# Token factors of three RMS norms taken out of the normalised rows and applied later: in gate and up of the two FFNs, and in the scale of the cross attention's exponential

## The chip, the core and the metric

The kernel runs on one core of one Trainium2 chip. The metric is device time in microseconds (us) of one execution. The core's engines work side by side and wait for one another by semaphores: TensorE (PE, matrix products into PSUM banks), VectorE (DVE), ScalarE (ACT), GpSimd (POOL), and SyncE (SP), which here issues almost all DMA transfers. Each engine runs its own instructions in the order in which they were written to its queue.

## What is computed

One layer of an encoder over 1088 tokens (1024 prompt frames and 64 frames of a running stream), 1024 features wide. Cut to what the change touches:

```python
def rmsnorm(x, g):
    xf = x.astype(F32)
    y = xf * lax.rsqrt(jnp.mean(xf * xf, axis=-1, keepdims=True) + EPS)
    return (y * g.astype(F32)).astype(x.dtype)

def swiglu(x, w_gu, w_d):
    gate, up = jnp.split(x @ w_gu, 2, axis=-1)
    return (jax.nn.silu(gate) * up) @ w_d

def ffn_half(x, g, w_gu, w_d):
    return x + 0.5 * swiglu(rmsnorm(x, g), w_gu, w_d)

def cross_attend(h, g_cross, w_cq, w_co, mk, mv):
    q = (rmsnorm(h, g_cross) @ w_cq).reshape(bsz, L, N_MEM_HEADS, MEM_HEAD_DIM)
    s = jnp.einsum('bqhd,bkhd->bhqk', q.astype(F32), mk.astype(F32)) * (MEM_HEAD_DIM ** -0.5)
    p = jax.nn.softmax(s, axis=-1)
    o = jnp.einsum('bhqk,bkhd->bqhd', p, mv.astype(F32)).reshape(bsz, L, D_MODEL)
    return o.astype(h.dtype) @ w_co

# per layer: ffn_half (FFN1), mixing (S5 group and differential attention, w_out),
# cross_attend into 256 memory tokens, ffn_half (FFN2), final rmsnorm
```

An RMS norm multiplies each token by one factor (the reciprocal root of its mean square) and each feature by one weight g. A matrix product over features is linear, so the token factor can be multiplied in before the product or after it.

## The kernel before

Activations lie with features on the 128 partitions: eight rows of 128x1088 (`row()`, one pool of 36 buffers) hold all tokens, in two column halves `TH[0]` and `TH[1]` of 544, called c = 0 and 1. Every product is made in fp32r from a high and a low part of each operand (`mm3`: high*high, high*low, low*high). A weight tile of 128x512 is cast on ACT (L154, and L155 for a rounded copy) and its low part subtracted on DVE (L156); an activation operand is cast on ACT (L343) and its low part made on DVE or POOL (L348).

**An FFN** (`ffn`) runs over 22 columns j of 128 hidden features. Per j, gate and up are made by seven products of half size in Strassen's manner, named b11, b21, t1, t2, t3, t4 and b22. Each is 24 matmuls of 272 columns, so 168 per j. b11, b21 and b22 take quarters of the input rows as they are; t1 to t4 take sums and differences of quarters, made on DVE (L338, class `Operands`). The weights of t1, t2, t3 and b22 are mixed on POOL (L605 to L608, `mixed`). `second()` adds the products into `gate` and `up` from PSUM (L580 on ACT, L585 on DVE) and on POOL (L635, L636), takes Silu of gate (L643, ACT), multiplies it into up (L644, POOL) and stores the row to `hid_d`. At an FFN's start the products b11 and b21 of the first `SKEWS` columns are made ahead of everything else, ten products where SKEWS is 5, while the operands of t1 to t4 are still being made. A side chain (`side`: in FFN1 the S5 parameters, `s5_prep`, and lambda) is advanced one step per product.

**Norm of FFN1.** Token tiles of x are loaded, squared and summed (`x_square`, L834 on ACT, L836 on DVE), and the factor is made per token (`half_rstd`, L218 to L230) and spread over all partitions by transposes of a broadcast column (L140 into L302, L303), giving the row `rb0`. Squares and factors stand ahead of all else in a hand-ordered block. Then, for each row and half, x is transposed on PE, copied to SBUF (`keep`, L863, L864) and multiplied by g and by rb0 in one DVE instruction (`x_norm`, L871).

**Norms 2 and 3** (class `Normed`: ahead of the cross attention, and ahead of FFN2). As the residual rows come out of the output projection's squares (`square`, steps n = 0 to 7), `add` squares them on ACT (L537) and sums them on POOL (L538). `finish(c)` makes sums over partitions with PE, then the factors, then the spread row. `get(k, c)` multiplies a row half by g and the spread row in place on DVE (L558): 16 for norm 2, 16 for norm 3. For norm 2, half c = 1 is normalised during `mem_proj` (the memory keys, L1658 on PE); the operands of w_cq's product follow (L425, L429, L454 on DVE). For norm 3, rows go to `Operands` of FFN2.

**Cross attention.** `c_scores` takes a maximum per token (L1753, L1754) and an exponential with the constant scale 1/16 (L1758).

Outside a few hand-ordered blocks, a tile scheduler sets each engine's order from its own timeline.

## Time and profile before

| | us |
|---|---|
| median of 3 runs | 2438.22 (2432.18 to 2440.07) |
| profiled execution | 2436.29 |
| its span, first to last instruction | 2434.5 |
| PE busy | 2272.9 (93%) |
| DVE busy | 1666.4 (68%) |
| ACT busy | 1287.2 (53%) |
| POOL busy | 1027.4 (42%) |

The mean granted TensorE clock was 0.977 of full speed. Busy shares are means over stages that differ: in the long middle of each FFN, PE is busy throughout; where a norm stands between two stages, PE stands idle in pieces. A row of the chain of waits or of a timeline that ends in square brackets gives the idle time of the engine just before that instruction and what ended it: "[8.52 <-DVE wl L156]" is 8.52 us until DVE wrote wl at line 156.

### The profile page before, as it was taken

The numbers are of one execution on the slowest core, as the hardware profiler recorded it, in microseconds if no ns is written. First come the engines' busy times: TensorE is split into PE (matmuls) and PEld (weight loads), VectorE is DVE, ScalarE is ACT, GpSimd is POOL, SyncE is SP. The second block draws the span as 40 slices with busy tenths as digits, with TensorE's granted clock in tenths as the row PEclk, the third lists the DMA queues.
The fourth block names the chain that finished last, engine by engine and source line by source line (L and its number), as shares of the span: only waits on it lengthen the run. The fifth ranks groups of instructions, "written<-read, shape, count | busy, mean of one in ns | idle before, by whom it ended". The sixth has DMA issues, their size and how long they took to land. (4 is left out here: it accounts for less than half of the span.)

```text
span 2434.5 us, 45373 instructions
## 1 busy us (share of the span) xinstructions
PE 2272.9 (93%) x16926; PEld 2207.6 (91%) x16926; DVE 1666.4 (68%) x3749; ACT 1287.2 (53%) x2511; POOL 1027.4 (42%) x801
## 2 busy tenths in 40 slices
PE   6899999999999998989989799987999999999998
PEld 6899999998999997978889799887999999998997
DVE  6557544358899696269978888789743333369897
ACT  6554444446555322267856566655554445464543
POOL 2666777754144200035335320355564445434340
PEclk9899999999999999999999999999999999999999
DMA  6232444443412425433443411133232222262312
GB/s 208 71 112 80 114 112 119 114 177 134 144 42 99 145 81 162 132 125 105 139 148 119 149 53 43 64 110 102 62 107 76 80 80 76 76 220 87 117 46 92
DMA packets 268295, 263.16 MB, mean 108 GB/s; under 512 B 36477, under 2 KB 217770, under 8 KB 268074
## 3 DMA queue, kind: packets, MB, share of 16 engines
q1 hardware_dynamic: 267984, 260.24, 33.6%
q8 instruction: 133, 2.18, 0.4%
q14 instruction: 88, 0.72, 0.1%
q10 hardware_dynamic: 90, 0.02, 0.0%
HBM read 187.03 MB, written 68.58 MB: 105 GB/s over the span
## 5 line engine op out<-in xcount | busy, mean ns | idle before, releaser
L174 PE MATMUL b<-r,wh 128*128 128x272 f32 (+4 forms) x9600 | 1690.6, 297 | 63.1 <-DVE r L709 14.5
L174 PEld LDWEIGHTS b<-r,wh 128*128 128x128 f32 x9600 | 1425.2, 192 | 79.8 <-DVE r L709 18.8
L174 PE MATMUL b<-r,wl 128*128 128x272 f32 (+4 forms) x4800 | 1055.0, 297 | 33.1 <-DVE wl L156 33.1
L174 PEld LDWEIGHTS b<-r,wl 128*128 128x128 f32 x4800 | 786.6, 191 | 37.3 <-DVE wl L156 37.0
L585 DVE TENSOR_TENSOR r<-b,r 128x272 f32<-128x272 f32 x440 | 172.2, 434 | 259.6 <-PE b L174 239.6
L156 DVE TENSOR_TENSOR wl<-wr,q 128x512 fp32r<-128x512 f32 x304 | 207.2, 682 | 192.7 <-ACT q L155 86.5
L154 ACT CAST wh<-wr 128x512 fp32r<-128x512 f32 x304 | 188.1, 622 | 248.6 <-PE b L174 224.8
L155 ACT CAST q<-wr 128x512 fp32r<-128x512 f32 x304 | 179.8, 591 | 259.7 <-DVE wl L156 257.4
L454 DVE TENSOR_TENSOR r<-r,r 128x544 fp32r<-128x544 f32 x224 | 213.2, 969 | 25.3 <-ACT r L453 24.2
L436 POOL TENSOR_TENSOR ws<-r,r 128x512 f32<-128x512 f32 x32 | 51.2, 1604 | 318.1 <-PE b L140 134.8
L154 ACT CAST wh<-ws 128x512 fp32r<-128x512 f32 x158 | 98.0, 621 | 137.6 <-PE b L174 114.6
L156 DVE TENSOR_TENSOR wl<-ws,q 128x512 fp32r<-128x512 f32 x158 | 107.5, 680 | 80.9 <-PE b L174 55.9
L155 ACT CAST q<-r 128x512 fp32r<-128x512 f32 x146 | 86.4, 592 | 124.0 <-DVE wl L156 123.7
L453 ACT CAST r<-r 128x544 fp32r<-128x544 f32 x224 | 143.8, 649 | 11.0 <-DMA r<-hid_d 6.5
L709 DVE SCALAR_TENSOR_TENSOR r<-b,r 128x272 f32<-128x272 f32 (+4 forms) x328 | 132.4, 438 | 22.2 <-PE b L174 21.2
L635 POOL TENSOR_TENSOR r<-r,r 128x544 f32<-128x544 f32 x44 | 61.4, 1395 | 195.8 <-DVE r L585 166.2
L155 ACT CAST q<-ws 128x512 fp32r<-128x512 f32 x158 | 93.8, 594 | 86.2 <-DVE wl L156 79.5
L156 DVE TENSOR_TENSOR wl<-r,q 128x512 fp32r<-128x512 f32 x146 | 99.5, 681 | 31.5 <-ACT q L155 30.2
L605 POOL TENSOR_TENSOR ws<-wr,wr 128x512 f32<-128x512 f32 x44 | 57.5, 1306 | 145.7 <-DMA wr<-w_ffn_gu 131.2
L1383 POOL CAST r<-r 64x256 fp32r<-64x256 f32 x32 | 13.6, 424 | 249.4 <-PE b L140 237.0
L644 POOL TENSOR_TENSOR r<-r,r 128x1088 f32<-128x1088 f32 x44 | 111.8, 2542 | 10.0 <-ACT r L643 10.0
L140 PE MATMUL b<-ident,r 128*128 128x128 f32 (+4 forms) x649 | 93.3, 281 | 19.8 <-DMA r<-g_subln 10.1
(323 smaller groups left out, 2942.3 us busy)
## 6 DMA issues: line engine op xcount, KB each, us to landing
wr<-w_ffn_gu SPq DMA_DIRECT2D x196, 256.0 KB, 2.9
hid_d<-r SPq DMA_DIRECT2D x44, 544.0 KB, 2.8
r<-hid_d SPq DMA_DIRECT2D x44, 544.0 KB, 6.7
h_d<-r SPq DMA_DIRECT2D x48, 272.0 KB, 2.4
r<-h_d SPq DMA_DIRECT2D x48, 272.0 KB, 2.8
r<-w_ffn_d SPq DMA_DIRECT2D x24, 512.0 KB, 7.1
wr<-w_in SPq DMA_DIRECT2D x32, 256.0 KB, 2.7
wr<-w_ffn_d SPq DMA_DIRECT2D x20, 256.0 KB, 2.8
```

The costliest lines, as they stand in the source:

```text
L140: T.transpose(out, in_, ident[:n, :n])
L154: A.copy(hi, x)
L155: A.copy(r, x)
L156: V.tensor_tensor(out=lo, in0=x, in1=r.bitcast(F32), op=ALU.subtract)
L174: T.matmul(pc[:, :c1 - c0], w, x[:, c0:c1], start=(first + i == 0 and q == 0), stop=(first + i == n - 1 and q == 2))
L453: A.copy(r[:, 0], v)
L454: V.tensor_tensor(out=r[:, 1], in0=v, in1=r[:, 0].bitcast(F32), op=ALU.subtract)
L585: V.tensor_tensor(out=oc, in0=pc, in1=tc_, op=ALU.add)
L605: G.tensor_tensor(out=s1, in0=r[2], in1=r[3], op=ALU.add)
L635: G.tensor_tensor(out=gate[:, T2], in0=gate[:, T2], in1=up[:, T2], op=ALU.add)
L644: G.tensor_tensor(out=up, in0=up, in1=gate, op=ALU.mult)
L709: V.scalar_tensor_tensor(out=hc_, in0=pc, scalar=0.5, in1=hc_, op0=ALU.mult, op1=ALU.add)
```

## The change

In FFN1, x_norm multiplies by g alone, with an instruction of one tensor operand. In norms 2 and 3, `get` multiplies by g alone, on ACT. The token factor is then applied:

- in both FFNs inside `second()`: up times the spread row `rb()` on POOL ahead of the product b22, and gate times it on DVE ahead of Silu, one instruction of 128x1088 each per j, 44 of each in all;
- in the cross attention as the scale of the exponential, per token (`by_tile` gives it as a 128x9 column set, from nine small products with ones; no spread row for norm 2).

With that, the factors are due later. FFN1's squares move out of the hand-ordered block into `x_start`, between the other steps, and the factors come after the operands of t1 and t2. Norm 2's `get` moves into steps 2, 5 and 6 of the square, the other four halves and `by_tile` into the background of mem_proj. Norm 3's rows become operands of b11 and b21 in steps 5 and 6; its factors come behind the operands of t1 and t2. SKEWS goes from 5 to 4 for both FFNs: eight products ahead instead of ten, and one gate row fewer, while the spread row is held through each FFN. The side chain of FFN1 takes lambda first.

```diff
-SKEWS = 5, 5
+SKEWS = 4, 4
...
-                V.scalar_tensor_tensor(out=x, in0=x, scalar=self.g[k], in1=self.rb[:, TH[c]], op0=ALU.mult, op1=ALU.mult)
+                A.activation(x, x, AF.Copy, scale=self.g[k])
             return self.rows[k]
 
-    def ffn(ops, w_gu, w_d, src_d, between, side=iter(()), ordered=False, on_row=None, on_chunk=None):
+        def by_tile(self):
+
+            ssq, acc = small([P, 9], "ssq"), self.acc.rearrange("p c n -> p (c n)")
+            V.memset(ssq, 1.0)
+            for t0, t1 in ((0, 4), (4, 8), (8, 9)):
+                p = bank()
+                for t in range(t0, t1):
+                    n = P if t < 8 else NS
+                    T.matmul(p[:n, (t - t0) * P:(t - t0 + 1) * P], acc[:, t * P:t * P + n], ones, start=True, stop=True)
+                n = P if t0 < 8 else NS
+                V.tensor_copy(ssq[:n, t0:t1], p.rearrange("p (t n) -> p t n", n=P)[:n, 0:t1 - t0, 0])
+            return rsqrt_mean(ssq, D, [P, 9], "rs")
+
+    def ffn(ops, w_gu, w_d, src_d, rb, between, side=iter(()), ordered=False, on_row=None, on_chunk=None):
...
             add(prod(w_split(r[3]), "t4"), up[:, T1])
+            G.tensor_tensor(out=up, in0=up, in1=rb(), op=ALU.mult)
             aside(j)
             yield
             add(prod(w_split(s[3]), "b22"), gate[:, T2])
             aside(j)
             yield
+            V.tensor_tensor(out=gate, in0=gate, in1=rb(), op=ALU.mult)
             A.activation(gate, gate, AF.Silu)
...
-        V.scalar_tensor_tensor(out=x0[k][:, TH[c]], in0=kept[k, c], scalar=g_ffn1[k], in1=rb0[:, TH[c]],
-                               op0=ALU.mult, op1=ALU.mult)
+        V.tensor_scalar(out=x0[k][:, TH[c]], in0=kept[k, c], scalar1=g_ffn1[k], scalar2=None, op0=ALU.mult)
...
-                if c == 0 and k in RS1_AT:
-                    next(rs1)
+                if c == 0 and k < 5:
+                    x_square(0, k, SQ_ACT[k])
+                elif c == 0 and k > 5:
+                    for t in ((0, 1, 2), (3, 4))[k - 6]:
+                        x_square(1, t, SQ_ACT[t])
             if c == 0:
                 yield
                 for k in range(X_AHEAD):
                     keep(k, 1)
+        for c in range(2):
+            yield from half_rstd(ssq0[c], rb0, c)
...
     def h2_norm():
         yield from steps(H2_PAUSE)
-        for _ in norm2.finish(1):
-            yield from steps(2)
-        for k in range(KT):
+        for k in range(4):
             norm2.get(k, 1)
-            if k % 2:
-                yield
+            yield
+        r = norm2.by_tile()
+        V.tensor_scalar(out=r, in0=r, scalar1=1.0 / 16, scalar2=None, op0=ALU.mult)
+        rs2.append(r)
...
-        A.activation(pe[:n], p[:n, :256], AF.Exp, bias=mx[:n], scale=1.0 / 16, accum_out=ss[:n])
+        A.activation(pe[:n], p[:n, :256], AF.Exp, bias=mx[:n], scale=rs, accum_out=ss[:n])
...
     def co_step(n, i):
-        if 4 * n + i in N0_AT:
-            next(n0, None)
-        if n == 6 and i:
-            ops3.get("b11", i - 1)
+        if n == 5:
+            ops3.get("b11", i)
+        if n == 6:
+            ops3.get("b21", i)
...
     def h_start():
-        yield from steps(H3_PAUSE)
-        yield from norm3.finish(1)
...
         ops3.low(*prev)
+        yield
+        for c in range(2):
+            yield from norm3.finish(c)
```

How the engines' own order changes, at three places. In these rows r, wh, wl, wr, ws, q and b are tiles with their numbers (r_97 is the spread row of FFN1), then the shape.

ACT at FFN1's start, before: seven squares (L834), then the first weight cast (L154) and the copies of the spread row (L302, L303).

```order
L834 ACTIVATE r_133,xq_119<-r_106 32x1024
L282 COPY gc<-b_89 128x45
L220 ACTIVATE rht_138<-rhv_135 128x5
L834 ACTIVATE r_146,xq_121<-r_108 128x1024
L834 ACTIVATE r_148,xq_121<-r_110 128x1024
L834 ACTIVATE r_150,xq_121<-r_117 32x1024
L154 CAST wh_201<-wr_199 128x512
L302 COPY r_97<-b_156 128x512
L303 COPY r_97<-b_157 128x32
```

The same engine now, around the first weight cast (L149), and some 20 instructions later:

```order
L845 ACTIVATE r_188,xq_119<-r_98 128x1024
L875 COPY r_195<-b_125 128x32
L874 COPY r_195<-b_190 128x512
L149 CAST wh_161<-wr_159 128x512
...
L338 CAST r_305<-r_303 128x544
L845 ACTIVATE r_308,xq_121<-r_108 128x1024
L845 ACTIVATE r_310,xq_121<-r_110 128x1024
L845 ACTIVATE r_312,xq_121<-r_112 128x1024
L215 ACTIVATE rht_714<-rhv_711 128x5
L150 CAST q_361<-wr_357 128x512
L338 CAST r_316<-r_314 128x544
```

Three copies of x and one operand cast now stand ahead of the first weight cast, and six squares stand behind it, among the weight casts and the operand casts of b11 and b21.

POOL in FFN1, where the columns j = 0 and 1 end their t4 and begin b22 (L348: low parts of operands, L605 to L608: weight mixes, L644: Silu's product), before:

```order
L348 TENSOR_TENSOR r_1124<-r_583,r_1124 128x544
L606 TENSOR_TENSOR ws_1084<-ws_1083,wr_1075 128x512
L607 TENSOR_TENSOR wr_1079<-wr_1075,wr_1079 128x512
L608 TENSOR_TENSOR ws_1085<-wr_1077,ws_1084 128x512
L348 TENSOR_TENSOR r_1189<-r_330,r_1189 128x544
L348 TENSOR_TENSOR r_1207<-r_349,r_1207 128x544
L605 TENSOR_TENSOR ws_1375<-wr_1371,wr_1373 128x512
```

And now (L343: low parts, L614 to L617: weight mixes, L647: the new product with the spread row):

```order
L343 TENSOR_TENSOR r_1051<-r_543,r_1051 128x544
L615 TENSOR_TENSOR ws_1011<-ws_1010,wr_1002 128x512
L616 TENSOR_TENSOR wr_1006<-wr_1002,wr_1006 128x512
L617 TENSOR_TENSOR ws_1012<-wr_1004,ws_1011 128x512
L647 TENSOR_TENSOR r_765<-r_765,r_97 128x1088
L647 TENSOR_TENSOR r_800<-r_800,r_97 128x1088
L343 TENSOR_TENSOR r_1118<-r_289,r_1118 128x544
L614 TENSOR_TENSOR ws_1306<-wr_1302,wr_1304 128x512
L615 TENSOR_TENSOR ws_1307<-ws_1306,wr_1298 128x512
L616 TENSOR_TENSOR wr_1302<-wr_1298,wr_1302 128x512
L617 TENSOR_TENSOR ws_1308<-wr_1300,ws_1307 128x512
L343 TENSOR_TENSOR r_1136<-r_314,r_1136 128x544
```

The two low parts of b22 that POOL makes stood back to back right behind the weight mixes; now two products with the spread row stand ahead of the first, and four further mixes ahead of the second.

DVE at the end of the memory keys' mem_proj (L156: low part of a weight; L425, L429: operands of w_cq), before:

```order
L156 TENSOR_TENSOR wl_16605<-wr_16602,q_16606 128x512
L558 SCALAR_TENSOR_TENSOR r_14715<-r_14715,gc,r_16052 128x544
...
L558 SCALAR_TENSOR_TENSOR r_14722<-r_14722,gc,r_16052 128x544
L156 TENSOR_TENSOR wl_16639<-wr_16636,q_16640 128x512
L425 TENSOR_TENSOR r_14715<-r_14715 128x544
```

And now (L151: low part of a weight; L449, L420, L424: operands of w_cq):

```order
L151 TENSOR_TENSOR wl_16546<-wr_16543,q_16547 128x512
L449 TENSOR_TENSOR r_16734<-r_14755,r_16734 128x544
L449 TENSOR_TENSOR r_16743<-r_14756,r_16743 128x544
L420 TENSOR_TENSOR r_14755<-r_14755 128x544
L449 TENSOR_TENSOR r_16752<-r_14757,r_16752 128x544
L420 TENSOR_TENSOR r_14756<-r_14756 128x544
L449 TENSOR_TENSOR r_16761<-r_14758,r_16761 128x544
L424 TENSOR_TENSOR r_14755<-r_14759,r_14755 128x544
L151 TENSOR_TENSOR wl_16581<-wr_16578,q_16582 128x512
```

The block of eight L558 between two weight tiles is gone, and operands of w_cq stand there.

## Rows read from the trace of the kernel before

**Rows 1.** The page's head and its first part: span, then busy time, share and instructions of each engine.

```profile
span 2434.5 us, 45373 instructions
PE 2272.9 (93%) x16926; PEld 2207.6 (91%) x16926; DVE 1666.4 (68%) x3749; ACT 1287.2 (53%) x2511; POOL 1027.4 (42%) x801
```

**Rows 2.** Busy time of each engine in one of twelve stretches of 40 us of FFN1, and the sum of the twelve, 120 to 600 us: the stretch and its length, then busy time (and instructions), granted clock, DMA share, GB/s.

```profile
240.00:280.00 40.00, 40.00 (x320) 39.78 (x319) 20.07 (x50) 19.64 (x38) 35.52 (x38) 1.00 0.36 96
...
sum 480.00, PE 473.16 PEld 467.55 DVE 262.31 ACT 244.46 POOL 308.53; mean PE 39.43 PEld 38.96 DVE 21.86 ACT 20.37 POOL 25.71
```

**Rows 3.** The same view of one stretch of FFN2's middle: columns PE, PEld, DVE, ACT, POOL as above.

```profile
1800.00:1840.00 40.00, 40.00 (x321) 40.00 (x320) 16.15 (x34) 19.17 (x37) 18.76 (x14) 1.00 0.26 82
```

**Rows 4.** The same view of FFN1's start, in stretches of 20 us.

```profile
20.00:40.00 20.00, 17.45 (x97) 15.12 (x97) 15.50 (x24) 19.05 (x48) 5.41 (x4) 1.00 0.61 198
40.00:60.00 20.00, 16.70 (x133) 15.94 (x132) 19.24 (x23) 10.94 (x28) 10.05 (x6) 1.00 0.44 148
```

**Rows 5.** ACT's timeline at FFN1's start: start, duration, line, operation, tiles and shape, count, and the idle time before it.

```profile
12.70 1.04 ACT L834 ACTIVATE r<-r 128x1024 f32<-128x1024 f32 x1
...
18.64 1.06 ACT L834 ACTIVATE r<-r 32x1024 f32<-32x1024 f32 x1 [3.77 <-DMA r<-x_sample]
...
19.70 0.60 ACT L154 CAST wh<-wr 128x512 fp32r<-128x512 f32 x1
...
36.72 0.66 ACT L343 CAST r<-r 128x544 fp32r<-128x544 f32 x1
```

**Rows 6.** PE's timeline at FFN1's start, with the waits of the argument.

```profile
13.68 1.35 PE L140 MATMUL b<-ident,rhy 128*128 128x128 f32 x5 [3.31 <-DVE rhy L230]
...
25.18 0.96 PE L174 MATMUL b<-r,wh 128*128 128x272 f32 x2 [1.12 <-ACT r L863]
...
107.75 0.82 PE L174 MATMUL b<-r,wh 128*128 128x272 f32 x2 [3.24 <-POOL r L348]
```

**Rows 7.** DVE's timeline at FFN1's start: single x_norm instructions (L871) of half c = 0, then of c = 1.

```profile
23.00 0.78 DVE L871 SCALAR_TENSOR_TENSOR r<-r,gc,r 128x544 f32<-128x544 f32 x1 [0.95 <-ACT r L864]
...
47.55 1.81 DVE L871 SCALAR_TENSOR_TENSOR r<-r,gc,r 128x544 f32<-128x544 f32 x1
...
65.83 0.77 DVE L871 SCALAR_TENSOR_TENSOR r<-r,gc,r 128x544 f32<-128x544 f32 x1
```

**Rows 8.** POOL's timeline: what it did around 47.55 us, and the start of the stretch from 91 to 113 us that it worked through without a pause.

```profile
47.01 1.77 POOL L607 TENSOR_TENSOR wr<-wr,wr 128x512 f32<-128x512 f32 x1
...
91.44 1.26 POOL L605 TENSOR_TENSOR ws<-wr,wr 128x512 f32<-128x512 f32 x1 [7.55 <-DMA wr<-w_ffn_gu]
```

**Rows 9.** Groups of instructions by line and shape: out<-in, count, then busy us and mean ns of one, then idle time before them and what ended it.

```profile
L644 POOL TENSOR_TENSOR r<-r,r 128x1088 f32<-128x1088 f32 x44 | 111.8, 2542 | 10.0 <-ACT r L643 10.0
...
L871 DVE SCALAR_TENSOR_TENSOR r<-r,gc,r 128x544 f32<-128x544 f32 x16 | 16.4, 1028 | 1.9 <-ACT r L864 1.2 <-ACT r L863 0.6
...
L208 DVE TENSOR_TENSOR r<-r,r 128x1088 fp32r<-128x1088 f32 x12 | 15.1, 1288 | 6.2 <-ACT r L207 6.2
...
L1785 DVE TENSOR_SCALAR ws<-ws,xr 128x256 f32<-128x256 f32 x32 | 10.9, 347 | 0.4
...
L1561 DVE TENSOR_SCALAR r<-r,rmy 128x1024 f32<-128x1024 f32 x2 | 1.4, 746 | 0.0
...
L1589 DVE TENSOR_TENSOR r<-r,r 128x1088 f32<-128x1088 f32 x4 | 9.7, 2419 | 3.8 <-ACT r L1587 3.8
...
L537 ACT ACTIVATE r<-r 128x544 f32<-128x544 f32 x28 | 18.1, 656 | 5.1 <-DVE r L505 4.4 <-POOL r L538 0.5
...
L643 ACT ACTIVATE r<-r 128x1088 f32<-128x1088 f32 x44 | 49.1, 1115 | 29.1 <-DVE r L585 28.9
```

**Rows 10.** DVE's timeline there; the first row is norm 2's other half, at 1346 us.

```profile
1346.32 7.52 DVE L558 SCALAR_TENSOR_TENSOR r<-r,gc,r 128x544 f32<-128x544 f32 x8
...
1382.19 10.69 DVE L558 SCALAR_TENSOR_TENSOR r<-r,gc,r 128x544 f32<-128x544 f32 x8
1392.81 0.68 DVE L156 TENSOR_TENSOR wl<-wr,q 128x512 fp32r<-128x512 f32 x1
...
1397.65 6.08 DVE L429 TENSOR_TENSOR r<-r,r 128x544 f32<-128x544 f32 x7
1403.66 0.67 DVE L156 TENSOR_TENSOR wl<-wr,q 128x512 fp32r<-128x512 f32 x1
```

**Rows 11.** PE's timeline there: the two waits for a weight's low part.

```profile
1393.54 0.58 PE L1658 MATMUL b<-r,wl 128*128 128x256 f32 x1 [8.52 <-DVE wl L156]
...
1404.39 0.82 PE L174 MATMUL b<-r,wl 128*128 128x272 f32 x2 [4.00 <-DVE wl L156]
```

**Rows 12.** Busy time by stretch, as in rows 2, from the end of w_co's product into FFN2.

```profile
1640.00:1680.00 40.00, 32.88 (x248) 30.71 (x247) 37.56 (x63) 24.48 (x44) 26.28 (x18) 1.00 0.28 93
1680.00:1720.00 40.00, 32.62 (x237) 31.53 (x237) 37.03 (x47) 17.13 (x37) 22.03 (x12) 0.91 0.24 69
1720.00:1760.00 40.00, 36.52 (x261) 35.49 (x260) 26.63 (x43) 23.66 (x42) 21.74 (x15) 0.91 0.23 66
```

**Rows 13.** Timelines of DVE and of PE there: norm 3's two blocks, and PE's longest wait.

```profile
1655.46 9.71 DVE L558 SCALAR_TENSOR_TENSOR r<-r,gc,r 128x544 f32<-128x544 f32 x8
...
1683.06 9.79 DVE L558 SCALAR_TENSOR_TENSOR r<-r,gc,r 128x544 f32<-128x544 f32 x8 [1.38 <-ACT r L303]
...
1703.11 0.82 PE L174 MATMUL b<-r,wh 128*128 128x272 f32 x2 [5.81 <-ACT r L580]
```

35 lines of the change are left out of this document (8 added, 27 removed).

## The prediction

> **What bounds the kernel now.** I read the page's busy shares first, then busy time by stretch, then in the stretches with gaps the timelines of PE and of the engine that its waits name. PE is busy for 2272.9 of 2434.5 us [rows 1], so no change to the other engines can give back much more than its 160 us of gaps, and only where the gaps are. In the middle of an FFN there are none: 320 or 321 matmuls in 40 us, 0.125 us each, with PE at 40.00 of 40.00 [rows 2, 3]. A column j of 168 matmuls takes 21 us there, and work that the change adds to DVE, ACT or POOL costs nothing while they keep up. The gaps that a norm can have to do with are at three places.
>
> FFN1's start: PE gets 97 and 133 instructions into two stretches of 20 us [rows 4], where 160 fit. First ACT is full (19.05 of 20), then DVE (19.24 of 20). Memory keys to w_cq: PE waits 8.52 and 4.00 us for a weight's low part [rows 11], which DVE makes only behind a block of eight norm instructions of 10.69 us and behind operands of w_cq [rows 10]. Cross attention's output to FFN2: DVE is busy 37.56 and 37.03 of 40 us while PE gets 248, 237 and 261 instructions into three stretches of 40 [rows 12]. By 0.125 us those 746 are 93 of 120 us, so 27 us are lost.
>
> **FFN1's start.** Removed from the path: the first transposes waited 3.31 us for the factors [rows 6], and the first weight cast stood behind the last square, which waited for its tile until 18.64 [rows 5]. The first product began at 25.18 [rows 6]. In the new order of ACT three rows are copied and one cast before that weight cast; if it still runs at 19.70, the product begins 0.6 us and a DVE subtraction of 0.7 later, about 20.8: a gain of 4.4.
>
> Given back on ACT: six squares now stand between the weight cast and the last cast of b11's and b21's operands. At 1.04 from start to start [rows 5] they take 6.2 to 6.9 us with their accumulator reads. Three copied rows, a cast and the spread row's copies leave that stretch, some 4 to 5 us. The last cast stood at 36.72, 17.0 us behind the first weight cast [rows 5]; I put it 1 to 2 us later. An engine that was busy 19.05 of 20 us [rows 4] has no room for this, so the earlier start is kept only in part. I count 1.5 against.
>
> DVE, 41 to 72 us: eight L871 of the second half go from 0.78 alone, 1.81 beside POOL [rows 7, 8], to a TENSOR_SCALAR. Between 0.347 for 256 elements and 0.746 for 1024 [rows 9] lies an estimate of 0.50 for 544. That saves 0.28 to 1.3 each, 2 to 5 in all if POOL's neighbourhood does not stretch the new one, nothing or a little if it does. The small factor instructions return 1. I take a gain of 2.
>
> Two leading products fewer are 48 matmuls, 6.0 us that PE could do while operands are made. They are only moved, and cost what PE then lacks: 0 to 6, I take 1. POOL, in order, now runs two products of 2.54 us [rows 9] ahead of b22's low part, for which PE already stood 3.24 us at t4 [rows 6]. The new order puts j = 2's t1 to t3 (9 us of PE work) between, so the price is 0 to 5; I take 1. Sum: -4.4 + 1.5 - 2 + 1 + 1, about **-3**; bounds -10 and +8.
>
> **Memory keys to w_cq.** Both DVE blocks of norm 2 go (7.52 and 10.69 us [rows 10]) to ACT, 16 instructions for which the nearest row is L537's 0.656 [rows 9], 10 us on an engine with idle time there. Named cover: ACT's own gaps at the square; if these are gone, the weight casts behind each are late by 0.6. Late next are the operands of w_cq, which DVE must still make; its row of 6.08 us [rows 10] still stands between weight tiles, as the new order shows, with nine small instructions of `by_tile`. So of 8.52 + 4.00 us I give back 9, with the slower clock in that gap in it. Bounds: all of 12.5 and the spread row's wait, -15; only a third, -3. **-9**.
>
> **Output of cross attention to FFN2.** 19.5 us of L558 [rows 13] leave DVE in 80 us in which it was busy 74.6 [rows 12]. ACT takes 16 scalings and has room (24.48 and 17.13 of 40 [rows 12]). The scaling overwrites rows that are being stored, so ACT, in order, waits for each store's landing with weight casts queued behind it; PE waits for those. PE's 5.81 us [rows 13] was ACT standing behind DVE's block, and goes. t1 to t4's operands come from the same DVE and ACT as before. I give back 11 of the 27 lost; -18 if DVE's whole relief arrives, -3 if ACT takes over its place and the two leading products fewer (6 us) are missed. **-11**.
>
> **Middle of the FFNs.** Added are 44 x 2.54 = 112 us on POOL and 44 products of 128x1088 on DVE, whose nearest rows are 1.29 and, beside POOL, 2.42 [rows 9]: 57 to 106 us. Per 40 us that is 4.8 on POOL and 2.5 to 4.6 on DVE, against 18.76 and 16.15 busy in FFN2 [rows 3]: hidden. In FFN1 one stretch has POOL at 35.52 of 40 [rows 2], which would become 40.4, but all twelve together 308.5 of 480 [rows 2], with the addition about 360. Behind POOL's product stand weight mixes that are made a column ahead, and behind DVE's stands ACT's Silu, which already waits 28.9 us for DVE [rows 9]. Its share of waiting may grow, with weight casts behind it. I take **+2**, bounds 0 and +10.
>
> The two engines' shared way to SBUF deserves a separate look. The same x_norm instruction took 0.78 us alone and 1.81 while POOL worked [rows 7, 8]. The Trainium skill, GPSIMD Engine Reference, section Key points, says that GpSimd shares its SBUF interfaces with VectorE and contends with DVE instructions of two SBUF inputs or in a two-port mode. By that rule all 44 new DVE products collide with POOL's 44, and the new one-operand x_norm too, so the DVE term goes to its upper bound and the gain of 2 at FFN1's start to nothing: the sum would be some 4 us smaller. The rows agree for two inputs; for one operand none shows it.
>
> **Sum.** -3 - 9 - 11 + 2 = -21 us against the profiled execution's 2436.29, span and the 1.8 us around it. The median of the runs is 2438.22, 1.9 above, so I forecast **2417** for the median. Other norms, the mixing stage and the FFNs' down products are untouched, and their terms nothing.
>
> **Rivals.**
> *ACT takes DVE's place.* Squares, 32 scalings of 0.656 (21 us) and their waits on stores land in an in-order queue that feeds PE's weights. For it: 19.05 of 20 [rows 4]. Against: 17 to 24 of 40 busy at norm 3 [rows 12]. Then FFN1's start gives back nothing or loses 2, and the two others a third each (-3, -4): -6 with the +2 and rounding, 2432.
>
> *POOL is late in FFN1; slower.* Decided where POOL's work exceeds 21 us per column: at 35.52 of 40 it had 18.6, with 2.54 it has 21.2. Then the next column's mixes slip, and DVE's additions behind them. If 10 of 22 columns lose 3 us, that is +30 against -23: about 2446. For it: that stretch; against: the sum of twelve [rows 2], and the scheduler may spread the S5 work, which has no due time there.
>
> *The leading products were the cover.* Where PE had ten, it has eight, and runs dry 6 us earlier at both FFNs: +12 on top of the sum, less the 1 counted: 2428.
>
> *More comes back.* DVE's relief passes whole to PE at all three places: -10 - 15 - 15 + 2 = -38, 2400.
>
> **How the numbers follow.** Forecast 0.52; ACT in DVE's place 0.18; POOL late 0.12; leading products 0.08; more 0.10. A measurement of this kernel can tell about 0.3%, 7.3 us, from no change: faster is below 2430.9, slower above 2445.5. Forecast, more and leading products are faster: 0.70. ACT in DVE's place is within: 0.18. POOL late is slower: 0.12. The range from 2397 to 2440 holds all but POOL late and the ends of the bounds; the forecast's own is 2408 to 2426.
>
> **What would show it.** Right: the first product near 21 us; no wait for wl above 5 us between 1340 and 1400; more than 800 instructions of PE in the 120 us around norm 3; PE at 320 per 40 us in the FFNs' middles with POOL near 24 of 40 in FFN2. Wrong: first operands after 37 us on an ACT without gaps; PE below 315 in FFN1's middle with waits for POOL; PE waiting for ACT's casts behind L554 at norm 3.

## The result, and the profile after

| | median us | runs |
|---|---|---|
| before | 2438.22 (2432.18 to 2440.07) | 5 |
| changed | 2448.89 (2447.60 to 2450.79) | 5 |

The ratio is 1.0051, with a 95% interval from 1.0035 to 1.0068: the change makes the kernel 0.5% slower, some 11 us, where 21 us less were forecast. The profiled spans say the same: 2447.1 us [rows 1: 2434.5], 12.6 more. The head of the page after:

```profile
span 2447.1 us, 45384 instructions
PE 2274.4 (93%) x16914; PEld 2202.3 (90%) x16914; DVE 1712.8 (70%) x3752; ACT 1310.8 (54%) x2540; POOL 1174.2 (48%) x845
```

To find where the 12.6 us arose, I took the first start of a few lines in both traces and subtracted the stages' lengths:

| from, to (first start of) | before | changed | difference |
|---|---|---|---|
| span's start, FFN1's first down residual | 546.4 | 563.9 | +17.5 |
| down residual, w_out's first block sum | 740.6 | 742.6 | +2.0 |
| block sum, first cross score maximum (norm 2) | 205.0 | 193.7 | -11.3 |
| score maximum, FFN2's Silu table load (norm 3) | 261.7 | 263.2 | +1.5 |
| table load, span's end (FFN2) | 680.8 | 683.7 | +2.9 |

The first row is read from the line of the down residual (L709 before, L720 after) in the view by line, whose columns are count, shortest, median and longest duration in ns, then first and last start:

```profile
L720 DVE SCALAR_TENSOR_TENSOR r<-b,r x328: 347/428/558, 563.9 to 2435.3; 128x272 f32<-128x272 f32 x136, 128x362 f32<-128x362 f32 x8, 128x256 f32<-128x256 f32 x8, 128x364 f32<-128x364 f32 x4
...
L151 DVE TENSOR_TENSOR wl<-wr,q x304: 664/678/746, 19.7 to 2347.0; 128x512 fp32r<-128x512 f32 x152
...
L594 DVE TENSOR_TENSOR r<-b,r x440: 415/431/443, 38.9 to 2167.4; 128x272 f32<-128x272 f32 x147
...
L653 DVE TENSOR_TENSOR r<-r,r x44: 1273/2322/2621, 120.5 to 2168.3; 128x1088 f32<-128x1088 f32 x44
```

(The other three lines are used below.) In four traces whose FFN1 is the same program, that of before, this first start is 546.4, 545.4, 545.2 and 542.7 us, so differences under 4 us in it say little.

So norm 2 gave what was forecast, norm 3 gave nothing, and FFN1 lost 17.5 us. Busy time by stretch, columns as in [rows 2]:

```profile
20.00:40.00 20.00, 17.12 (x93) 14.41 (x94) 14.25 (x27) 20.00 (x48) 5.41 (x4) 0.74 0.47 161
40.00:60.00 20.00, 17.22 (x133) 16.74 (x132) 19.97 (x30) 12.70 (x33) 11.12 (x7) 0.96 0.54 172
...
160.00:200.00 40.00, 36.54 (x285) 35.70 (x284) 38.37 (x77) 18.04 (x34) 25.19 (x14) 1.00 0.18 54
200.00:240.00 40.00, 36.99 (x280) 36.17 (x279) 26.87 (x49) 17.84 (x34) 31.02 (x43) 0.96 0.29 86
240.00:280.00 40.00, 36.68 (x289) 35.93 (x288) 16.01 (x32) 18.77 (x37) 37.99 (x41) 1.00 0.36 98
280.00:320.00 40.00, 38.14 (x299) 36.95 (x299) 20.62 (x35) 17.86 (x34) 33.61 (x30) 1.00 0.39 100
...
120.00:600.00 480.00, 463.55 (x3630) 456.40 (x3628) 287.01 (x505) 240.38 (x458) 362.96 (x287) 0.99 0.39 120
...
1650.00:1690.00 40.00, 34.89 (x264) 34.04 (x263) 33.99 (x54) 33.25 (x60) 29.26 (x20) 0.96 0.26 90
1690.00:1730.00 40.00, 33.23 (x242) 32.09 (x242) 20.39 (x46) 17.57 (x37) 10.70 (x9) 0.91 0.23 67
1730.00:1770.00 40.00, 35.01 (x255) 33.31 (x254) 27.77 (x38) 21.52 (x37) 33.08 (x20) 0.96 0.25 73
...
1800.00:1840.00 40.00, 40.00 (x321) 40.00 (x320) 19.89 (x35) 20.31 (x37) 28.43 (x17) 1.00 0.32 100
```

FFN1's start is as tight as before [rows 4], with ACT now at 20.00 of 20 and a granted clock of 0.74. From 160 to 320 us PE has 285, 280, 289 and 299 matmuls where 320 fit, while POOL over the twelve stretches has 362.96 us, almost the 360 of the forecast. FFN2's column, with the same two products, runs at 321 [rows 3]. Around norm 3 DVE now has room in the middle stretch (20.39 of 40, 37.03 in [rows 12]), but PE's 264, 242 and 255 are hardly more than the 248, 237 and 261 of before. PE's waits say who is late:

```profile
19.19 0.77 PE L169 MATMUL b<-r,wh 128*128 128x272 f32 x4 [1.17 <-ACT wh L149]
...
167.55 0.65 PE L169 MATMUL b<-r,wh 128*128 128x272 f32 x3 [1.59 <-DVE r L594]
172.36 0.65 PE L169 MATMUL b<-r,wh 128*128 128x272 f32 x3 [1.53 <-DVE r L594]
...
202.84 0.23 PE L135 MATMUL b<-ident,r 16*128 16x16 f32 x1 [2.03 <-DVE r L1008]
...
204.05 0.35 PE L135 MATMUL b<-ident,r 16*128 16x16 f32 x3 [0.98 <-DVE r L1009]
...
247.85 0.52 PE L169 MATMUL b<-r,wh 128*128 128x272 f32 x2 [1.79 <-ACT r L1109]
...
278.08 0.65 PE L169 MATMUL b<-r,wh 128*128 128x272 f32 x3 [1.30 <-ACT r L589]
...
293.26 0.65 PE L169 MATMUL b<-r,wh 128*128 128x272 f32 x3 [0.81 <-DVE r L1146]
...
313.13 0.64 PE L169 MATMUL b<-r,wh 128*128 128x272 f32 x3 [1.05 <-DVE r L594]
...
1401.68 0.39 PE L1662 MATMUL b<-r,wl 128*128 128x256 f32 x1 [1.82 <-DVE wl L151]
...
1409.49 0.58 PE L1662 MATMUL b<-r,wl 128*128 128x256 f32 x1 [2.24 <-DVE wl L151]
...
1686.61 0.58 PE L541 MATMUL b<-ones,r 128*32 128x128 f32 x2 [4.79 <-ACT r L589]
...
1698.51 1.35 PE L135 MATMUL b<-ident,rhy 128*128 128x128 f32 x5 [6.77 <-DVE rhy L225]
```

The first product starts at 19.19 [rows 6: 25.18]. Behind the memory keys no wait for a weight's low part is above 2.24 us [rows 11: 8.52 and 4.00]. At norm 3 PE stands 11.6 us at the two steps of `finish`: the sums (L541) and the transposes of the factors (L135). They stand in PE's queue directly behind the leading products for which the operands of t1 and t2 are made.

In FFN1 PE stands ten times between 145 and 330 us, 11.6 us together (0.7 before). 6.0 us of it are for the additions and copies that empty a product's PSUM banks (L594 on DVE, L589 on ACT), and 5.6 are the side work's: its transposes wait for L1008 and L1009, and products behind it for the copies L1109 and L1146 out of its PSUM tiles. No wait there names a weight's low part or a mix. DVE's timeline around three of these waits, then POOL's at the same times:

```profile
166.34 0.67 DVE L151 TENSOR_TENSOR wl<-wr,q 128x512 fp32r<-128x512 f32 x1
...
168.08 2.51 DVE L986 TENSOR_SCALAR r<-r 16x128 f32<-16x128 f32 x1
170.52 1.30 DVE L988 TENSOR_SCALAR r<-r 16x128 f32<-16x128 f32 x1
171.75 0.21 DVE L987 TENSOR_SCALAR r<-r 16x128 f32<-16x128 f32 x1
171.88 0.77 DVE L594 TENSOR_TENSOR r<-b,r 128x272 f32<-128x272 f32 x2
...
200.34 2.45 DVE L1008 TENSOR_TENSOR r<-r 16x128 f32<-16x128 f32 x1
202.82 1.17 DVE L1009 TENSOR_SCALAR r<-r 16x128 f32<-16x128 f32 x1
```

```profile
167.99 2.53 POOL L647 TENSOR_TENSOR r<-r,r 128x1088 f32<-128x1088 f32 x1 [2.53 <-DVE r L594]
170.47 1.27 POOL L614 TENSOR_TENSOR ws<-wr,wr 128x512 f32<-128x512 f32 x1
...
200.12 2.52 POOL L655 TENSOR_TENSOR r<-r,r 128x1088 f32<-128x1088 f32 x1
202.61 1.31 POOL L617 TENSOR_TENSOR ws<-wr,ws 128x512 f32<-128x512 f32 x1
```

L986, L988 and L987 are instructions of the state-space parameters, all 16x128. L987 took 0.21 us; L986, the same operation, took 2.51 and ended at 170.59, L988 ended at 171.82, each within 0.1 us of POOL's instruction beside it (170.52 and 171.74). At 202.8 and 204.0 it is nearly so (within 0.15 us). DVE is in order, so what stands behind them is late: the addition L594 at 171.88, for which PE waited 1.53 us at 172.36, and the transposes of L1008's and L1009's results at 202.84 and 204.05. The weight lows (L151) are late too, and ACT, also in order, stands at the cast for the next low, whose tile q DVE has not yet read:

```profile
205.38 0.59 ACT L150 CAST q<-ws 128x512 fp32r<-128x512 f32 x1 [5.90 <-DVE wl L151]
```

ACT stands so in the other versions too: from 145 to 240 us 33.6 us in the changed kernel, 27.3 before, 28.5 to 29.5 in e1 and e2 below. So this wait does not tell them apart.

I went into the experiments with this as **theory A**: the added products, POOL's above all, fill and stretch DVE's queue in FFN1's middle. Its rivals were **B**, eight leading products instead of ten, and **C**, the new order of the side work (lambda's parameters first). For norm 3: the place of the factors, or the operands' queue on DVE. A rival that I did not name: whatever is edited, the tile scheduler sets the order of the rest anew.

### The profile page after: what moved, and what is told of

The parts are those of the page before. It is cut to its first block, busy times and chain, and to the rows that moved or that the text cites. A ratio compares the mean times of both kernels' runs of the same rounds, so it can differ in the third digit from the quotient of the medians.

```text
span 2447.1 us, 45384 instructions
## 1 busy us (share of the span) xinstructions
PE 2274.4 (93%) x16914; PEld 2202.3 (90%) x16914; DVE 1712.8 (70%) x3752; ACT 1310.8 (54%) x2540; POOL 1174.2 (48%) x845
## 5 line engine op out<-in xcount | busy, mean ns | idle before, releaser
L594 DVE TENSOR_TENSOR r<-b,r 128x272 f32<-128x272 f32 x440 | 172.5, 433 | 256.7 <-PE b L169 198.0
L151 DVE TENSOR_TENSOR wl<-wr,q 128x512 fp32r<-128x512 f32 x304 | 206.9, 680 | 151.8 <-issue 69.5
L149 ACT CAST wh<-wr 128x512 fp32r<-128x512 f32 x304 | 188.0, 622 | 214.2 <-PE b L169 188.7
L449 DVE TENSOR_TENSOR r<-r,r 128x544 fp32r<-128x544 f32 x224 | 214.5, 975 | 25.0 <-ACT r L448 24.4
L151 DVE TENSOR_TENSOR wl<-ws,q 128x512 fp32r<-128x512 f32 x158 | 107.5, 680 | 91.2 <-PE b L169 48.7
L149 ACT CAST wh<-ws 128x512 fp32r<-128x512 f32 x158 | 98.0, 621 | 119.3 <-PE b L169 103.9
L720 DVE SCALAR_TENSOR_TENSOR r<-b,r 128x272 f32<-128x272 f32 (+4 forms) x328 | 132.3, 437 | 23.3 <-PE b L169 22.3
L644 POOL TENSOR_TENSOR r<-r,r 128x544 f32<-128x544 f32 x44 | 61.5, 1398 | 161.6 <-DVE r L594 122.8
L647 POOL TENSOR_TENSOR r<-r,r 128x1088 f32<-128x1088 f32 x44 | 112.0, 2547 | 37.2 <-DVE r L594 37.2
L151 DVE TENSOR_TENSOR wl<-r,q 128x512 fp32r<-128x512 f32 x146 | 99.4, 681 | 35.4 <-ACT q L150 34.4
L655 POOL TENSOR_TENSOR r<-r,r 128x1088 f32<-128x1088 f32 x44 | 112.7, 2562 | 7.0 <-ACT r L654 7.0
L135 PE MATMUL b<-ident,r 128*128 128x128 f32 (+4 forms) x649 | 93.0, 281 | 21.4 <-DMA r<-x_prompt 10.8
```

The source lines that it names most:

```text
L135: T.transpose(out, in_, ident[:n, :n])
L149: A.copy(hi, x)
L151: V.tensor_tensor(out=lo, in0=x, in1=r.bitcast(F32), op=ALU.subtract)
L449: V.tensor_tensor(out=r[:, 1], in0=v, in1=r[:, 0].bitcast(F32), op=ALU.subtract)
L594: V.tensor_tensor(out=oc, in0=pc, in1=tc_, op=ALU.add)
L644: G.tensor_tensor(out=gate[:, T2], in0=gate[:, T2], in1=up[:, T2], op=ALU.add)
```

## The experiments

Ratios are to the kernel before, measured beside it on the same chip (its medians there were 2435 to 2437 us), with 95% intervals. "Residual" is the first down residual of FFN1 (before 546.4, changed 563.9 us). Eight medians fell in none of the ranges expected of them: those of e1, e7, e8, e12, e13, e14, e15 and e16.

| run | median us | ratio | residual |
|---|---|---|---|
| e1, no factor in FFN1 | 2424.95 | 0.9953 (0.9941 to 0.9965) | 541.8 |
| e2, no factor on up | 2432.24 | 0.9982 (0.9972 to 0.9992) | 547.1 |
| e3, no factor on gate | 2443.91 | 1.0036 (1.0023 to 1.0048) | 554.9 |
| e4, side order back | 2442.45 | 1.0025 (1.0015 to 1.0035) | 565.7 |
| e5, norm 2 alone | 2426.69 | 0.9954 (0.9940 to 0.9968) | 545.4 |
| e6, norms 2 and 3, late factors | 2418.77 | 0.9924 (0.9912 to 0.9936) | 545.2 |
| e7, parameters spread | 2445.23 | 1.0034 (1.0022 to 1.0046) | 562.6 |
| e8, up's factor on DVE | 2442.11 | 1.0018 (1.0010 to 1.0027) | 556.7 |
| e9, norms 2 and 3 as changed | 2428.02 | 0.9952 (0.9938 to 0.9965) | 542.7 |
| e10, changed, late factors | 2442.99 | 1.0020 (1.0012 to 1.0029) | 565.8 |
| e11, up's factor in halves | 2444.11 | 1.0028 (1.0019 to 1.0037) | 556.4 |
| e12, before, eight leading | 2443.08 | 1.0020 (1.0010 to 1.0030) | 551.4 |
| e13, halves interleaved | 2459.55 | 1.0091 (1.0074 to 1.0108) | 572.5 |
| e14, factor at column's end | 2460.01 | 1.0102 (1.0084 to 1.0120) | 567.6 |
| e15, e12 with new side order | 2439.59 | 1.0011 (1.0002 to 1.0019) | 544.9 |
| e16, e14 with late factors | 2450.48 | 1.0067 (1.0050 to 1.0083) | 565.6 |
| e17, state products on DVE | 2450.37 | 1.0064 (1.0048 to 1.0080) | 566.7 |
| e18, e17 with e11 and e10 | 2442.34 | 1.0028 (1.0019 to 1.0038) | 562.4 |

**Which part of FFN1 costs: e1 to e4.** In e1 both lines run in FFN2 only, in e2 the first, in e3 the second.

```diff
+            if on_row is None:
-            G.tensor_tensor(out=up, in0=up, in1=rb(), op=ALU.mult)
+                G.tensor_tensor(out=up, in0=up, in1=rb(), op=ALU.mult)
...
+            if on_row is None:
-            V.tensor_tensor(out=gate, in0=gate, in1=rb(), op=ALU.mult)
+                V.tensor_tensor(out=gate, in0=gate, in1=rb(), op=ALU.mult)
```

> The changed kernel with both products by the token factors left out of FFN1's columns (gate and up of the first FFN are not normalised by token; FFN2's stay). Theory A, the added products fill VectorE's and GpSimd's queues in FFN1's middle, where VectorE is held while GpSimd works: the 17 us that FFN1's middle lost come back, 2430 to 2436 us, and the first down residual of FFN1 stands near 547 us of the trace instead of 564. Rival B, the middle lost them because only eight leading products stand ahead of it and the side work began a column earlier: 2446 to 2450 us, residual still near 562. Rival C, the order of the side work (lambda's parameters ahead of the state-space parameters): the same 2446 to 2450 us.

> The changed kernel with GpSimd's product of up by the token factors left out of FFN1's columns, VectorE's product of gate kept. Theory A with GpSimd's product as the holder: two thirds or more of the 17 us come back, 2432 to 2440 us, and VectorE's product of gate falls from 2.3 us median to 1.3 to 2 us. If it is VectorE's own added 1,088 columns that count: at most a third comes back, 2444 to 2449 us. Rivals B and C: 2446 to 2450 us.

> The changed kernel with VectorE's product of gate by the token factors left out of FFN1's columns, GpSimd's product of up kept. Theory A with GpSimd as the holder: a third or less comes back, 2442 to 2448 us, and the small state-space instructions on VectorE still end with GpSimd's products. If VectorE's own added work counts: most comes back, 2432 to 2440 us. Rivals B and C: 2446 to 2450 us.

e4 puts the side work's order back:

```diff
-chain(diff_lambda(), s5_params(), ...
+chain(s5_params(), diff_lambda(), ...
```

> The changed kernel with the side work of FFN1's columns in the order of the kernel before (the state-space parameters first, lambda's after them). Rival C, the order made the chain late: 2434 to 2444 us. Theory A: 2446 to 2451 us, no change that can be told. Rival B: the same 2446 to 2451 us.

e1's residual is at 541.8: without the two products 22.1 us come back there, all that FFN1 lost, and FFN1 is no longer than before (542.7 to 546.4). POOL's product is worth 16.8 (e2), DVE's 9.0 (e3); alone, without the other, 13.1 (554.9 - 541.8) and 5.3 (547.1 - 541.8). e4 leaves the residual where it was (565.7): C is out for FFN1. Its median is in C's range even so, some 6 us under the changed kernel's; these arose behind FFN1, in pieces that I cannot place.

Where in FFN1 the time goes is told by the starts of its Silus (ACT; L643 before), one for each column j, in us:

| column | 4th | 5th | 12th | 22nd |
|---|---|---|---|---|
| before | 148.5 | 163.6 | 320.6 | 541.1 |
| changed | 145.1 | 174.5 | 336.9 | 558.5 |
| e1 | 138.1 | 161.5 | 312.8 | 536.5 |
| e2 | 145.9 | 167.6 | 319.9 | 543.7 |
| e3 | 143.1 | 170.7 | 326.0 | 547.4 |
| e15, below | 141.4 | 164.8 | 316.0 | 539.6 |

Behind the twelfth column next to nothing is lost. Of the 22.0 us between e1 and the changed kernel, 7.0 are there at the fourth Silu already, before the middle. What DVE's product costs alone (e2 against e1) is all there by then, 7.8 us, and does not grow; what POOL's costs on top of it (changed against e2) arises wholly between the fourth and the twelfth. At the start the engines' orders differ too: POOL adds a first sum (L644) at 84.29 us in e1, ahead of its first weight mix, and at 90.58 us in the changed kernel, behind four mixes, as in e2. Of POOL's 191 other instructions ahead of 345 us in the changed kernel, 153 can be found in the same order in e1, 166 in e2 and 178 in e3. So e1 and e2 leave out a product and change the order, and no run here parts the two.

**Norms 2 and 3: e5, e6, e9, e10.** e5 is the kernel before with the change's lines of norm 2 alone. e9 adds norm 3 and FFN2 as the change has them, e6 is e9 with the factors written later, and e10 is the changed kernel with that same edit:

```diff
         yield
-        for c in range(2):
-            yield from norm3.finish(c)
+        yield
+        f = [norm3.finish(c) for c in range(2)]
+        for c in (0, 1, 0, 1):
+            next(f[c])
+            yield
```

> The kernel before with the change's cross attention norm alone (weights on ScalarE, factors by tile into the exponential's scale); both FFNs as before. If the 9 to 11 us that the landmarks of the changed kernel give back between the memory keys and the cross attention belong to this part: 2425 to 2429 us beside 2436 to 2438 of before. If they were only there because FFN1 ended late and transfers had caught up: 2433 to 2440 us.

> The kernel before with the change's cross attention norm and its FFN2 norm, FFN1 as before, and norm 3's token factors written later: first the sums of both halves, then the two transposes, one leading product between each. If the 6.8 us that TensorE stood at the factors' transposes were what ate the gain of norm 3: 2417 to 2424 us, and no wait over 3 us at those transposes. If the wait belongs to the operands' queue on VectorE and only moves to another instruction: 2425 to 2431 us, as with norm 2 alone or a little over it.

> The kernel before with the change's norms 2 and 3 and FFN2, FFN1 as before, and norm 3's token factors where the change has them. It differs from the run with late factors by their place alone. If that place ate norm 3's gain: 2424 to 2430 us beside 2436 to 2438 of before, with a wait of 5 us or more at the factors' transposes. If the 8 us between the earlier two runs came from elsewhere: 2417 to 2422 us.

> The changed kernel whole, with norm 3's token factors written later (sums of both halves, then both transposes, a leading product between each). The place of the factors: 2438 to 2443 us, 6 to 10 us under the changed kernel. If the wait only moves: 2446 to 2450 us.

e5 came at 10.7 us less: norm 2's gain is its own. From the first score maximum to FFN2's table load e5 takes 264.9 us (1479.2 to 1744.1), e9 263.7 (1475.3 to 1739.0), e6 253.6 (1479.1 to 1732.7); e10 takes 254.7 (1502.9 to 1757.6) against the changed kernel's 263.2. The place of the factors alone is 10.1 and 8.5 us (the same stretch, with norm 3 as it was, took 261.7 before and 264.9 in e5). PE's waits at L546 and L140 (there the lines of the sums and of the transposes) in e9:

```profile
1660.97 0.41 PE L546 MATMUL b<-ones,r 128*32 128x128 f32 x2 [4.79 <-ACT r L597]
...
1672.86 1.35 PE L140 MATMUL b<-ident,rhy 128*128 128x128 f32 x5 [6.74 <-DVE rhy L230]
```

and in e6, where both have all but gone:

```profile
1667.78 0.41 PE L546 MATMUL b<-ones,r 128*32 128x128 f32 x2 [0.91 <-DVE r L602]
...
1676.50 0.79 PE L140 MATMUL b<-ident,rhy 128*128 128x128 f32 x5 [0.70 <-DVE rht L228]
```

e6 is also the fastest version found, 0.9924 of before.

**The leading products: e12 and e15.** The kernel before with `SKEWS = 4, 5` instead of `5, 5`, and the same with the changed order of the side work.

> The kernel before with eight leading products in FFN1 instead of ten (the first constant of the two alone). Rival B, the leading products were the cover of FFN1's middle: 8 to 17 us slower than before, 2445 to 2455 us. Theory A: within 3 us of before, 2433 to 2441 us.

> The kernel before with eight leading products in FFN1 and the changed order of the side work (lambda's parameters first). If the 5 us that FFN1 lost with eight leading products came from the burst of state-space parameters falling into the first columns: 2434 to 2439 us, first down residual 544 to 548 us. If fewer leading products cost it whatever the order: 2441 to 2446 us, residual near 551 us.

Eight products with the old order lose 5.0 us at the residual (551.4); with the new order it is at 544.9, nothing lost that shows there, though e15's median is still 2.8 us above that of before. So B has some weight where the state-space parameters come first, which the change avoids, and little else of FFN1's 17.5 us. The two products that are no longer made ahead are seen in the table above: from the fourth Silu to the fifth e15 takes 23.4 us, before 15.1; e15 is level again at the end. e1 is e15 with the changed FFN1 start and the other two norms: 541.8 against 544.9, which is under the 4 us that say little.

**How the products cost it: e7, e8, e11, e13, e14, e16, e17, e18.** e7 spreads the parameters' instructions over four more steps (the expectation says five):

```diff
-        yield from steps(4)
+        yield from steps(2)
...
         e = tmp[:, 7]
+        yield
         exp_small(x, e)
+        yield
...
+        yield
         lim = 3.1415925
...
         A.activation(th, s, AF.Sin)
+        yield
...
-        yield from steps(4)
+        yield from steps(2)
```

> The changed kernel with the state-space parameters' small VectorE instructions spread over five more steps of the side work (their number, and all of the steps, as before). Theory A in the form that a burst of small instructions, each held to the end of a GpSimd instruction, is what made the weight lows late: half or more of FFN1's 17 us back, 2436 to 2442 us. If VectorE and GpSimd are late from the sum of all their work in these columns, whatever its order: 2446 to 2451 us.

e8 puts the product of up on DVE:

```diff
-            G.tensor_tensor(out=up, in0=up, in1=rb(), op=ALU.mult)
+            V.tensor_tensor(out=up, in0=up, in1=rb(), op=ALU.mult)
```

> The changed kernel with the product of up by the token factors on VectorE instead of GpSimd, in both FFNs. Theory A with GpSimd's instructions as holders: FFN1's middle gets back 10 us or more in spite of 18 more VectorE products in it, 2434 to 2441 us, and VectorE's products take 1.3 to 2 us each. If VectorE's own queue is the limit: slower still, 2449 to 2460 us.

e11 cuts it in halves by column, and e13 in halves of even and odd elements, with `h_::2` in the place of `TH[h_]`:

```diff
-            G.tensor_tensor(out=up, in0=up, in1=rb(), op=ALU.mult)
+            for h_ in range(2):
+                G.tensor_tensor(out=up[:, TH[h_]], in0=up[:, TH[h_]], in1=rb()[:, TH[h_]], op=ALU.mult)
```

> The changed kernel with GpSimd's product of up by the token factors written as two of 544 elements each instead of one of 1,088. Theory A, a VectorE instruction is held until GpSimd's current instruction ends: the holds behind this product are half as long and a quarter to a half of FFN1's 17 us comes back, 2440 to 2446 us. If it is the sum of GpSimd's work that counts, the same or a little more: 2447 to 2452 us.

> The changed kernel with GpSimd's product of up by the token factors in two halves that are interleaved (even and odd elements), so that both wait for the t4 add as the whole did. If the length of the instruction that VectorE is held behind counts: as with the halves by column, 2440 to 2446 us, first down residual near 556 us of the trace. If the wait in GpSimd's queue counts: nothing back, 2446 to 2452 us, residual 562 to 567 us.

e14 moves the product, so that it no longer waits for t4's sum in front of the next column's mixes (POOL stood 2.53 us so at 167.99, above); e16 adds the late factors:

```diff
-            G.tensor_tensor(out=up, in0=up, in1=rb(), op=ALU.mult)
...
             G.tensor_tensor(out=up, in0=up, in1=gate, op=ALU.mult)
+            G.tensor_tensor(out=up, in0=up, in1=rb(), op=ALU.mult)
```

> The changed kernel with GpSimd's product by the token factors behind the product of up and gate instead of ahead of it: as many and as long GpSimd instructions, but none of them waits for the t4 add in front of the next column's mixes; the order of GpSimd's queue has the four mixes ahead of both products from the fifth column on. If the wait in the queue counts: 8 us or more of FFN1's 17 back, residual 545 to 556 us, 2432 to 2441 us. If the hold of VectorE behind GpSimd's work counts: a third at most, residual 558 to 566 us, 2443 to 2451 us.

> The changed kernel with GpSimd's factor product at the column's end and norm 3's factors written later. The mends add if they are of different stages: by the queue theory 2424 to 2434 us; by the hold theory 2436 to 2444 us. The kernel before with norms 2 and 3 alone and the late factors stays ahead of it at 0.992 of before unless FFN1's middle ends under 545 us.

e17 gives both instructions of `scaled`, in `s5_prep`, to `V` instead of `G`; e18 adds the edits of e11 and e10.

> The changed kernel with the state-space products of powers (some 1.0 to 1.2 us each on GpSimd, from 250 us of the trace on, none before) on VectorE instead of GpSimd. If FFN1's second stretch, 240 to 320 us, is lost because GpSimd is full there: PE goes from 289 and 299 matmuls in its two windows to 310 or more each, while 160 to 240 us stays as it was (285 and 280), and 4 to 7 us come back: 2441 to 2445 us. If VectorE is the limit of both stretches: nothing back or slower, 2447 to 2456 us.

> The changed kernel with the state-space products on VectorE, GpSimd's factor product in two halves by column, and norm 3's factors written later. If the three are of different stretches and add: 5 to 7 us, 4 to 5 us and 6 us under the changed kernel's 2448 to 2450, that is 2430 to 2435 us, under the kernel before. If two of them are paid from the same stretch: 2437 to 2443 us.

Matmuls that PE had in four stretches of 40 us, from the view by stretch, and the sum of PE's waits from 145 to 330 us, from the view of waits:

| | 160 to 200 | 200 to 240 | 240 to 280 | 280 to 320 | PE's waits, us |
|---|---|---|---|---|---|
| before | 321 | 316 | 320 | 312 | 0.7 |
| changed | 285 | 280 | 289 | 299 | 11.6 |
| e1 | 316 | 305 | 321 | 320 | 1.5 |
| e2 | 318 | 319 | 322 | 319 | 0.2 |
| e3 | 295 | 297 | 305 | 319 | 5.3 |
| e7 | 256 | 321 | 289 | 300 | 9.6 |
| e8 | 286 | 284 | 313 | 314 | 6.3 |
| e11 | 273 | 308 | 293 | 319 | 6.7 |
| e13 | 272 | 273 | 288 | 306 | 12.3 |
| e14 | 263 | 293 | 277 | 319 | 13.6 |
| e17 | 285 | 274 | 280 | 294 | 13.1 |

The runs with the longer waits are nearly those with the later residual.

e8: with both products on DVE, which adds work to the fuller engine, 7.2 us come back (556.7). A DVE that is short of time by its own work alone would have lost more; POOL's product costs beyond its own length. e7: the burst's loss moves into one stretch (256) and out of the next (321), and the sum stays: this order does not help.

e14 takes the wait out of POOL's queue (8.1 us at L647 in the changed kernel from 145 to 330 us, none in e14), the residual stays at 567.6, and FFN2 is longer besides (695.3 us from table load to end, against 683.7, in an execution 7 us above e14's median; 688.2 in e16): that queue theory falls, and e16, which adds the late factors, came out above both of its ranges. e17 takes POOL from 37.99 and 33.61 us busy to what these rows show, and PE gets nothing for it:

```profile
240.00:280.00 40.00, 35.66 (x280) 34.89 (x279) 25.63 (x44) 18.61 (x37) 25.45 (x28) 1.00 0.34 94
280.00:320.00 40.00, 37.64 (x294) 36.23 (x293) 28.81 (x45) 13.41 (x26) 23.52 (x19) 1.00 0.42 107
```

So a POOL that is full is not by itself the limit of the second stretch. But e17 is not a clean test: it gives the work to DVE, whose additions empty PE's banks. And POOL is late there in the changed kernel. DVE's additions (L594) stand behind POOL's sums of gate and up (L644, L645):

```profile
263.01 0.79 DVE L594 TENSOR_TENSOR r<-b,r 128x272 f32<-128x272 f32 x2 [5.10 <-POOL r L644]
...
287.40 1.48 DVE L594 TENSOR_TENSOR r<-b,r 128x272 f32<-128x272 f32 x4 [5.38 <-POOL r L645]
...
312.63 1.48 DVE L594 TENSOR_TENSOR r<-b,r 128x272 f32<-128x272 f32 x4 [5.92 <-POOL r L645]
```

From 240 to 320 us these waits for POOL are 20.9 us in the changed kernel, 13.3 before, 4.2 in e1 and 4.9 in e17. In e3 they are 19.1, with 2.0 us of waits left on PE from 240 to 330 (5.2 in the changed kernel), so they alone do not settle it either. e11 had 7.5 us back, but in e18 the same halves gave 4.3 over e17 (562.4 against 566.7), little more than the landmark's spread, and e13's cost 8.6 more. e13's are also longer, at their shortest 1587 ns for the same 544 elements that take e11's 1338:

```profile
L648 POOL TENSOR_TENSOR r<-r,r x88: 1587/1610/3470, 108.5 to 2179.1; 128x544 f32<-128x544 f32 x88
```

```profile
L648 POOL TENSOR_TENSOR r<-r,r x88: 1338/1362/2432, 100.7 to 2161.7; 128x544 f32<-128x544 f32 x88
```

The length of the single POOL instruction is therefore not isolated by these runs. Most of what e18 has over e17 are the late factors: it takes 252.1 us from score maximum to table load (1502.9 to 1755.0), e17 263.8 (1501.4 to 1765.2).

What the hold amounts to can be estimated: for all DVE instructions between 120 and 360 us, the durations less count times the shortest duration of that operation and shape in these traces. That is 28.7 us before, 39.1 in the changed kernel, 39.2 in e3 (POOL's product alone), 31.0 in e2 (DVE's alone), 31.5 in e1. POOL's product adds some 8 us of hold to DVE (39.1 - 31.0, 39.2 - 31.5), about half of the 16.8 us that it is worth at the residual. DVE's own adds no hold, only its length, some 12 x 1.27 = 15 us in that time. How 8 us of hold on DVE become 16.8 on PE is not shown.

## Why the prediction was wrong

**FFN1's start, -3: right in its pieces, not shown as a sum.** The first product came at 19.19 (near 21 forecast), and x_norm's instruction takes 0.497 us (0.50 forecast):

```profile
L882 DVE TENSOR_SCALAR r<-r,gc x16: 490/497/1153, 13.9 to 62.1; 128x544 f32<-128x544 f32 x16
```

But at 120 us the changed kernel has had no more matmuls than the kernel before (592 each), and at the fourth Silu it is 3.7 us behind e15, which has the old start and as many leading products. e1, without the two products, is 3.3 us ahead of e15 there. Both are about what the same program differs by (145.0 to 148.5 us in four traces).

**Memory keys to w_cq, -9: right.** -11.3 by landmarks, -10.7 alone (e5); the waits that it was read from are at 2.24 us and less.

**Output of cross attention to FFN2, -11: failed, at one step.** DVE was relieved as forecast, and 8.1 us come back with the factors later (261.7 before, 253.6 in e6), 11.3 against e5. The step "PE's 5.81 us was ACT standing behind DVE's block, and goes" missed that the change also moves the factors. They left the stretch ahead of the operands, and their sums and transposes now stand in PE's in-order queue just behind the products that wait for t1 and t2, at 4.79 and 6.77 us. The first of these waits names the same copy on ACT as the 5.81 us did (L589, L580 before): that wait did not go, it moved to the sums. For the second, the factors' small instructions stand among the operands in DVE's queue, from 1687.5 to 1698.5 us. I costed what left DVE and did not follow `finish` to its new place on PE; e6 and e9 show that this place took the gain. The scalings on ACT were no part of it: 744 ns each (0.656 us forecast), and 0.6 us of waiting for stores in all.

**Middle of the FFNs, +2, bounds 0 and +10: failed.** It was +22.1 in FFN1 (changed against e1), and 1.5 to 2.9 in FFN2 (e6 and the changed kernel, from table load to end). FFN2's sum was right, and the step that failed is "hidden" for FFN1. The argument went by sums over twelve stretches, which came out as forecast, and by POOL's mixes. What e1 to e3 show is that FFN1 is longer with either product in it and that POOL's costs more. Between 160 and 200 us the late queue is DVE's: it is busy 38.37 of 40, with the parameters' chain, the gate product and the holds in the same queue as the additions that empty PE's banks, and PE waits for these additions and for the chain's own results. From 240 us on, where DVE is busy 16.01 of 40, it stays open through what chain the products cost PE its 53 matmuls (588 against 641 in e1 and in e2): DVE's additions stand there behind POOL's sums, and PE's waits name what empties its banks. POOL's wait for t4's sum (e14) is not the reason, POOL's fullness alone is not (e17), and without POOL's product the loss is gone (e2: 322 and 319). Some 7 of the 22.1 us lie ahead of the middle, where the engines' order differs as well.

The rule of the Trainium skill that I weighed (GPSIMD Engine Reference, section Key points: contention with DVE instructions of two SBUF inputs or in a two-port mode) bears on it, and the trace agrees with it: L653, with two SBUF inputs, goes to 2621 ns from 1273, and L986, with one, to 2.51 us from 0.21. x_norm, with one, goes to 1153 from 490. Which mode these two ran in no trace shows. L151 and L594, each with one input in PSUM, are never above 746 and 443 ns in the rows above. I priced it at 4 us, on the new instructions alone. The estimate of the hold puts twice that on instructions that the change does not touch, the parameters ahead of PE's additions, beside which POOL now works longer.

**The rivals.** *POOL is late in FFN1* had the sign and nearly the time (2446 forecast; its own terms, +30 against -23, give 2445), but not the mechanism: no wait of PE in the middle is for a mix, and moving POOL's product away from the mixes (e14) gained nothing. That POOL's sums are late for DVE from 240 us on is as near as it came. *The leading products were the cover*: at most 5.0 us, with the old side order (e12, e15). *ACT takes DVE's place* is seen in one place, ACT at 20.00 of 20 from 20 to 40 us, and e1, which has it too, shows no loss from it. *More comes back* did not occur.

Open, then: what the new order costs by itself and what the products cost; the second stretch's chain; why halves by column helped in e11 and hardly in e18; and e4's 6 us.

## What to carry to other kernels

A product that is nearly hidden in one stage (FFN2, nothing beside it) need not be hidden in the same loop with side work on the same two engines: read the busiest stretch and its queue, not the sum over the loop. When a norm's factor is taken off the path, follow its own matmuls and transposes to their new place in PE's queue; here that place decided 8 to 10 us, and one more leading product between each step mended it. When one instruction is left out to see what it costs, compare the other engines' orders too: a scheduler may have moved them. Scaling by token inside an instruction that is there anyway was cheap (the exponential of norm 2's stage went from 474 to 565 ns in the median, and the stage still gave 11 us back); a product of its own per column cost FFN1 its time.
